# Gate and up begin with eight products of the first token half instead of four, in a fused encoder block on one Trainium2 core

## The chip, the core and the metric

The kernel runs on one core of a Trainium2 chip. The core has five engines, each with a queue of its own that it works off in order: TensorE (PE in the profile, and PEld for its weight loads), VectorE (DVE), ScalarE (ACT), GpSimd (POOL) and SyncE (SP), which here only issues DMAs. The engines meet through semaphores alone: an instruction that waits holds up everything behind it in its own queue. Matmuls write to PSUM, which has eight banks of 128 x 512 fp32; everything else lies in SBUF.

The metric is the device time of one launch in microseconds, a median over runs; lower is better.

## The reference, cut to what matters

```python
def reference(x, ...):                      # x: (1, 1024, 1024) float32
    h = rms_norm(x, norm1_g)
    z = h @ w_in                            # conv value and gate, q, k, v
    conv_out = conformer_conv(a, gate, ...) # 31 taps, layer norm, silu
    attn_out = neighbourhood_attention(rms_norm(q), rms_norm(k), v, rpb)
    x = x + concat([conv_out, attn_out]) @ w_out
    h = rms_norm(x, norm2_g)
    return x + (silu(h @ w_gate) * (h @ w_up)) @ w_down   # d_ff = 2816
```

The change touches the end of `@ w_out` and above all the beginning of the last line: the second norm and the two products `h @ w_gate` and `h @ w_up`.

## The kernel before, in words

All matmuls of fp32 data run as three products of fp32r halves. `split` (L106) makes the halves: ScalarE casts the source into `hi` (L107), and VectorE or GpSimd subtracts, `lo = src - hi` (L111); the argument `sub` says which of the two. `mac` (L113) then issues hi x hi, hi x lo and lo x hi (L115 to L117).

The text of the kernel is the order of the work. There is no scheduler: each engine's queue is what the Python calls append to it, and where work of one kind is to stand between matmuls, functions are put in the list `woven`, from which `weave()` takes one after each group of three matmuls.

**Output projection.** `proj` (L808) sums eight groups for one unit (m, h): eight row blocks m of the output, two token halves h of 512 tokens. Raw weights arrive by DMA in tiles of the tag R (`R`, L85; three buffers), are split by `take` (L152), and the order of loads is the list `chunks` (L137). `resid` (L865) adds the residual on VectorE and stores the result to DRAM by SP. `square`, `token_sums` and `token_rows` (L967 to L986) make the second norm's scale for a token half: squares on ScalarE, sums on GpSimd, a sum over partitions and a transpose on TensorE. `norm2` (L988) applies it on VectorE, reading the scale from PSUM.

**Gate and up, as Strassen-Winograd.** The product has 22 blocks i of 128 columns; for each, seven products m1 to m7 take the place of eight. One product (`product`, L1216) is four `mac`s, 12 matmuls of 512 columns. The weights of a block are raw tiles `raw_gu[i, 0]` and `raw_gu[i, 1]` (`load_gu`, L995, two DMAs of 512 KB), their sums `t_sums` (L1000, four VectorE sums) and the splits of the seven operands (`prep`, L1134). The token side has operands that all blocks share: A11 and A12 are the two halves of the normed first token half (`h2`); S3, A22, S2, S1 and S4 need the second token half. `left` (L1171) makes one of these for a k: a VectorE sum or difference in place in `xT` (L1179) and a split. For blocks 0 and 1 the seven products of both blocks are taken pair by pair, in the order of the list `products` (L1012): m1, m2 (only A11, A12), then m7 (S3), m4 (A22), m6 (S2), m5 (S1), m3 (S4). The other blocks follow one by one (L1017).

Products add up in PSUM banks: bank A takes m1 and m2, bank D m7 and m4, bank B m6, m5 and m3. Between two products of a bank, `evac` (L1241) reads the partial sum out on VectorE or ScalarE, so the next product into the same bank waits for that sum. The one for m6 is `u2` (L1249), for m7 and m5 L1258, for m3 L1262.

From block 4 on m1 (from block 6 on m2 too) is itself done by seven quarter products for two blocks at once (`part`, L1098; `prep_part`); the token operands for it are made beside the early products on GpSimd and VectorE by `tok_full`, `tok_sum` and `tok_split`, at product numbers given by the table `TOK` (L1091).

The loop at L1369 runs over `products`. After product n and its `evac` it calls `after[n]` (L1363), which holds the norm of the second half and `left`, and then `prep`, which takes tasks in the order of their numbers. As engines work in order, what `after[n]` appends stands ahead of what `prep` appends after it: a cast for a weight on ScalarE stands behind the casts of `left` issued in the same step.

Of the kernel before, what the change touches and what calls it, by code (L numbers as in the profile page):

```python
# [12 lines left out]
P = 128  # L13
# [57 lines left out]
def build(ctx, tc, a):  # L71
# [7 lines left out]
    def T(tag, shape, bufs, name, dt=F32):  # L79
        return sb.tile(shape, dt, tag=tag, bufs=bufs, name=name)  # L80
# [2 lines left out]
        return T("G", [P, 1024], 21, name, dt)  # L83

    def R(name):  # L85
        return T("R", [P, 1024], 3, name)

    def H(name, dt=F32):
        return T("H", [P, 4096], 7, name, dt)
# [2 lines left out]
        return T("st", [P, 512], 5, name, dt)  # L92

    def SM(name, n=8):
        return T("sm", [P, 8], 16, name)[:, :n]

    def mm(name):
        return ps.tile([P, 512], F32, tag="mm", bufs=4, name=name)
# [20 lines left out]
    def lr(w):  # L119
        return w[:, :512], w[:, 512:]  # L120
# [90 lines left out]
    def wo_dst(d, k0):  # L211
        def dst():
            if (d, k0 // 4) == (1, 1):
                if not woq:
                    woq.append(H(f"wo{d}{k0}", F32R))
                o = k0 % 4 * 1024
                hl = (woq[0][:, o:o + 1024], woq[0][:, o + 1024:o + 2048])
            else:
                hl = (G(f"wo{d}{k0}h", F32R), G(f"wo{d}{k0}l", F32R))
            for j in range(2):  # L220
                wo[d, k0 + j] = [w[:, j * 512:(j + 1) * 512] for w in hl]
            return hl
        return dst

    for d in range(2):
        for k0 in (4, 6, 0, 2):
            want(a["wo"][k0 * P:(k0 + 2) * P, d * 512:(d + 1) * 512].rearrange("(k p) m -> p k m", p=P),
                 f"wo{d}{k0}", wo_dst(d, k0), (pool,) * 4 if d == 0 and k0 < 4 else (pool,))


    hT = [[H(f"hT{h}{w}", F32R).rearrange("p (k s) -> p k s", s=512) for w in range(2)] for h in range(2)]
# [721 lines left out]
    for h, ms_ in ((0, range(4)), (1, (0, 1))):  # L953
        for k in CONV:
            for m in ms_:
                proj(m, h, (k,), None, 1 + (m + 1) % 2)
        for m in ms_:
            resid(m, h)
        if h == 0:
            take(2)  # L960
    for m in range(6, 8):
        load_xT(m)
    take(2)

    ssum, rn, rows = {}, {}, {}

# [42 lines left out]

    ORDER = ("m1", "m6", "m7", "m2", "m5", "m4", "m3")  # L1010
    ms = [m + h * QF for m in range(QF) for h in range(2)]
    products = [(i, p) for p in ("m1", "m2", "m7", "m4", "m6", "m5", "m3") for i in range(2)]  # L1012
    PARTS = {"m1": {-7: ("P1", "P6"), -5: ("P2", "P5", "P7"), -3: ("P3", "P4")},
             "m2": {-1: ("P1", "P6"), 0: ("P2", "P5", "P7"), 2: ("P3", "P4")}}
    FIRST_I = {"m1": 4, "m2": 6}
    parted = lambda i, p: i >= FIRST_I.get(p, FB)
    products += [(i, p) for i in range(2, FB) for p in ORDER if not parted(i, p)]  # L1017

# [4 lines left out]
            for o, g in at_.items() if parted(i, m) else ():  # L1025
                parts_at.setdefault(n0 + o, []).append((m, i, g))
    LEAD = {"load": 2, "P1": -2, "P6": -2, "P7": -2, "P4": -1}
    tasks = [(n, ip) for n, ip in enumerate(products)]
    for n, gs in parts_at.items():
        for m, i, g in gs:  # L1030
            tasks += [(n - LEAD[q] - 0.5, (m, i, q)) for q in (("load",) if "P1" in g else ()) + g if q in LEAD]
# [50 lines left out]
    def tok_split(m, n):  # L1082
# [3 lines left out]
        else:  # L1086
# [1 line left out]
            tok4[m, n] = [t[:, 0], t[:, 1]]  # L1088
        split(*tok4[m, n], tok_raw[m, g][:, c], (pool,))

    TOK = {6: (tok_full, "m1", 0), 8: (tok_full, "m1", 3), 9: (tok_full, "m1", 2), 10: (tok_full, "m1", 1),  # L1091
           11: (tok_sum, "m1", 1), 12: (tok_sum, "m1", 3), 15: (tok_sum, "m1", 2), 16: (tok_split, "m1", 2),
           17: (tok_sum, "m1", 4), 19: (tok_split, "m1", 1), 20: (tok_split, "m1", 3), 21: (tok_split, "m1", 4),
           22: (tok_full, "m2", 0), 23: (tok_full, "m2", 3), 25: (tok_full, "m2", 1), 27: (tok_full, "m2", 2),
           28: (tok_sum, "m2", 1), 30: (tok_sum, "m2", 3), 31: (tok_split, "m2", 3), 32: (tok_sum, "m2", 2),
# [38 lines left out]
    def prep(n=1, upto=None):  # L1134
        while tasks and (n > 0 if upto is None else tasks[0][0] <= upto):
            n -= 1
            job = tasks.pop(0)[1]
            if len(job) == 3:
                prep_part(*job)
                continue  # L1140
            i, p = job
            if i > 1 and p == ("m6" if parted(i, "m1") else "m1"):
                t_sums(i, (1, 2))
            elif i > 1 and p == ("m7" if parted(i, "m1") else "m6"):
                t_sums(i, (3, 4))
            b = {"m1": (0, 0), "m2": (0, 1), "m3": (1, 1)}.get(p)
            m = {"m5": 0, "m6": 1, "m7": 2, "m4": 3}.get(p)
            src = lr(raw_gu[i, b[0]])[b[1]] if b else lr(tsum[i, m // 2])[m % 2]
            top[i, p] = lr(G(f"t{i}{p}", F32R))
            split(*top[i, p], src, (dve,) if i < 2 and p in ("m1", "m2", "m6", "m5") else (pool,))  # L1150
            if (i, p) == (0, "m2"):
                load_gu(1, 1)
            if (i, p) == (1, "m7"):
                load_gu(2, 0)
            if (i, p) == (0, "m3"):
                load_gu(2, 1)
            if (i, p) == (1, "m3"):
                load_gu(3, 0)
            if i > 1 and p == ("m7" if parted(i, "m2") else "m2"):
                load_gu(i + 1, 1)  # L1160
            if i > 1 and p == "m3":
                load_gu(i + 2, 0)


    sop = {}
# [17 lines left out]
        norm2(k, 0)  # L1183
        split(h2[0][:, k], h2[1][:, k], xT[k][:, :512])

    for i, j in ((0, 0), (0, 1), (1, 0)):
        load_gu(i, j)

    units = [(m, 0) for m in range(4, 8)] + [(m, 1) for m in range(2, 8)]
    for m in range(4):  # L1190
        square(m, 0)
    beside = {(2, 5): [lambda: token_sums(0)], (3, 1): [lambda: token_rows(0)],
              (4, 5): [lambda: t_sums(0, (1, 2))], (5, 5): [lambda: t_sums(0, (3, 4))],
              (7, 3): [lambda: t_sums(1, (1, 2))], (7, 5): [lambda: t_sums(1, (3, 4))]}
    for kb, at_ in enumerate(((3, 3), (3, 7), (4, 3), (4, 7), (5, 3), (5, 7), (6, 3), (6, 7))):
        beside.setdefault(at_, []).append(lambda kb=kb: h2_one(kb))
    for m, h in units:
# [13 lines left out]

    sd = dr.tile([QF, P, 7 * 512], F32, name="sd")
    LEFT = {"m1": "A11", "m2": "A12", "m3": "S4", "m4": "A22", "m5": "S1", "m6": "S2", "m7": "S3"}
    gt, bank, sl, u2, late = {}, {}, {}, {}, []

    def product(i, p):  # L1216
        w = {"m1": "A", "m2": "A", "m7": "D", "m4": "D"}.get(p, "B")
        alone = p == "m2" and parted(i, "m1")
        first = p in ("m1", "m6", "m7") or alone
        if alone:  # L1220
            if i % 2 == 0:
                pair_sl[0] = lr(cv(f"A{i}"))
            bank[i, w] = pair_sl[0][i % 2]
        elif first:
            bank[i, w] = (tp if w == "D" and i > 1 else mm)(f"{w}{i}")
        acc, (th, tl), s = bank[i, w], top.pop((i, p)), sop[LEFT[p]]
        for k in range(HK):
            mac(acc, [q[:, k * P:(k + 1) * P] for q in (th, tl)], [s[h][k] for h in range(2)],
                k == 0 and first, k == HK - 1)
            weave()  # L1230
        return acc
# [9 lines left out]
    def evac(i, p, acc):  # L1241
        if p == "m1":
            gt[i] = G(f"g{i}")
        l, r = lr(gt[i])
        if p == "m1":
            (act.copy if i else dve.tensor_copy)(l, acc)
        elif p == "m6":
            u2[i] = ST(f"u2{i}")
            dve.tensor_tensor(u2[i], acc, l, OP.add)  # L1249
            if i < 2:  # L1250
                gate2(i, bank[i, "D"])
        elif p == "m2":
            sl[i] = ST(f"sl{i}") if i < 2 else acc
            if parted(i, "m1"):
                dve.tensor_tensor(acc, acc, l, OP.add)
            act.activation(sl[i], acc, AF.Silu)
        elif p in ("m5", "m7"):
            dve.tensor_tensor(r, acc, l if p == "m7" else r, OP.add)  # L1258
            if i < 2 and p == "m5":
                up2(i, r, bank[i, "D"])  # L1260
        elif p == "m3":
            dve.tensor_tensor(l, acc, l, OP.add)  # L1262
            dve.tensor_tensor(l, sl[i], l, OP.mult)
            keep(i, 0, l)
        elif i > 1:
            gate2(i, acc)
            late.append(lambda: up2(i, r, acc))
# [89 lines left out]
    def prep_items(n):  # L1357
        for _ in range(n):
# [1 line left out]
            n_prep[0] += 1  # L1360


    after = {0: lambda: (token_sums(1), act.activation(warm, eps, AF.Silu)),  # L1363
             1: lambda: [(norm2(k, 1), left("S3", k)) for k in range(HK)],
             2: lambda: [(norm2(k + HK, 1), left("A22", k)) for k in range(HK)],
             3: lambda: [left("S2", k, dve) for k in range(HK)],
             5: lambda: [left("S1", k) for k in range(HK)],
             7: lambda: [left("S4", k) for k in range(HK)]}
    for n, (i, p) in enumerate(products):  # L1369
        if n == 1:  # L1370
            woven.extend([lambda: None, lambda: token_rows(1)])
        pacc = product(i, p)
        evac(i, p, pacc)
        if n in after:
            after[n]()
        if late and p != "m4":
            late.pop(0)()
        due = extra and p in ("m2", "m5", "m7", "m6", "m3")[:5 if parted(i, "m2") else 4]
        if due and not parted(i, "m1"):
            extra.pop(0)()  # L1380
        for m, i0, g in parts_at.get(n, ()):
            for q in g:
                part(m, i0, q)
        if n < 6:
            prep((1, 1, 1, 1, 1, 1)[n])
        else:
            prep(upto=n + 4)
        if due and parted(i, "m1"):
            extra.pop(0)()
        if n in TOK:  # L1390
            TOK[n][0](*TOK[n][1:])
        if i == FB - 1 and p == "m7":
            for q in range(4):
                load_item(q)
        if i == FB - 1 and p in ("m5", "m4", "m3"):
            prep_items(1 + (p == "m5"))
# [103 lines left out]
```

## Time and profile before

| | |
|---|---|
| median of 3 runs | 1056.51 us (1055.28 to 1057.07) |
| the profiled execution: its time | 1057.38 us |
| the profiled execution: its span, first to last instruction | 1055.7 us |
| mean granted TensorE clock | 0.988 of full speed |
| TensorE busy | 1031.6 us, 98% |
| VectorE busy | 777.8 us, 74% |
| GpSimd busy | 490.5 us, 46% |
| ScalarE busy | 477.6 us, 45% |

The page of the profile has busy times by engine, and the span in 40 equal slices: a digit is the busy share of a slice in tenths, in the row PEclk the granted clock. The timelines list instructions of one engine by start and duration in us, with line, output and input tiles by the program's names; in brackets is the idle time just before, and what ended it. The table of waits lists which engine waited for which line of which other, in all, how often, and the longest. Matmuls are pipelined: one of 512 columns takes 0.39 us from start to end, and the next starts 0.23 us after it.

### The profile page before, as it was taken

To read this page: it belongs to the slowest core of one execution; us is meant where nothing else is said; L and a number is where in the kernel's file an instruction comes from. 1 tells how busy PE (TensorE), PEld (TensorE's weight loads), DVE (VectorE), ACT (ScalarE), POOL (GpSimd) and SP (SyncE) were. 2 spreads that over 40 slices of the span, in tenths; PEclk is the share of its full clock that TensorE was granted. 3 is DMA by queue.
4 is the path that set the end of the run, shared out by engine and by line. 5 is a ranking of instruction groups with operands and counts; after the bars stand their busy time and mean duration, and the time that the engine had idled before them with its cause. 6 is when DMAs were issued, how large, how long until landed. Compare 5 with 4: busy or idle time off the path is not lost.

```text
span 1055.7 us, 15166 instructions
## 1 busy us (share of the span) xinstructions
PE 1031.6 (98%) x5334; PEld 859.2 (81%) x5334; DVE 777.8 (74%) x1200; ACT 477.6 (45%) x1044; POOL 490.5 (46%) x380
## 2 busy tenths in 40 slices
PE   9999999999999899689999999999999999999998
PEld 8888888877787687468888888888888888888887
DVE  5789997887754157887778877877787667857885
ACT  7465349737865234324243333433333444433432
POOL 1036755524641545687786675666667200002320
PEclk9999999999999999789999999999999999999999
DMA  9335781338222512023343344434333598623641
GB/s 350 152 89 186 226 256 40 120 111 269 62 97 95 198 41 70 1 75 126 120 150 131 101 151 146 148 122 146 130 105 130 190 340 288 210 81 119 208 152 50
DMA packets 75084, 152.53 MB, mean 144 GB/s; under 512 B 13824, under 2 KB 22784, under 8 KB 74368
## 3 DMA queue, kind: packets, MB, share of 16 engines
q1 hardware_dynamic: 72992, 148.21, 41.7%
q10 hardware_dynamic: 2016, 3.36, 0.9%
q8 instruction: 42, 0.69, 0.3%
q14 instruction: 34, 0.28, 0.1%
HBM read 112.38 MB, written 44.76 MB: 149 GB/s over the span
## 4 chain that ended last, share of the span: by engine, by line
PE 88%; DVE 7%; ACT 2%; POOL 1%; issue 1%; DMA 1%; DVEq 0%; ACTq 0%; POOLq 0%
PE B L115 5%; PE B L116 5%; PE B L117 5%; PE z L115 4%; PE z L117 4%; PE z L116 4%; PE D L115 3%; PE D L116 3%; PE D L117 3%; PE gl L115 3%; PE gl L117 3%; PE gl L116 3%; PE p L720 2%; PE o L739 2%; PE s L680 2%; PE pj L117 2%
## 5 line engine op out<-in xcount | busy, mean ns | idle before, releaser
L363 DVE SCALAR_TENSOR_TENSOR cv<-u,par,cv 128x1009 f32<-128x1009 f32 (+14 forms) x92 | 117.4, 1277 | 2.3
L389 POOL TENSOR_TENSOR pa<-pa,pr 128x1022 f32<-128x1022 f32 (+5 forms) x24 | 58.0, 2416 | 48.4 <-ACT pr L388 35.8
L1443 POOL TENSOR_TENSOR ou<-ou,resm 128x512 f32<-128x512 f32 x8 | 12.6, 1582 | 143.5 <-DMA resm<-xd 141.6
L107 ACT CAST op<-sr 128x512 fp32r<-128x512 f32 x77 | 47.6, 619 | 58.1 <-PE B2d L117 26.7
L111 DVE TENSOR_TENSOR op<-sr,op 128x512 fp32r<-128x512 f32 x77 | 58.1, 755 | 16.3 <-ACT op L107 16.3
L709 POOL TENSOR_SCALAR e<-e,rs 128x288 f32<-128x288 f32 (+1 forms) x64 | 33.9, 545 | 41.9 <-DVE rs L707 40.1
L1007 DVE TENSOR_TENSOR ts<-gu,ts 128x512 f32<-128x512 f32 x44 | 51.9, 1181 | 0.8
L107 ACT CAST op<-wd 128x512 fp32r<-128x512 f32 x54 | 33.4, 619 | 29.1 <-DVE wd L1345 18.5
L698 ACT ACTIVATE e<-e,mx 128x288 f32<-128x288 f32 (+1 forms) x64 | 36.5, 572 | 18.8 <-DVE mx L693 16.9
L111 DVE TENSOR_TENSOR op<-wd,op 128x512 fp32r<-128x512 f32 x54 | 41.3, 764 | 1.2
L693 DVE CUSTOM_DVE_ANT_0 e<-s,tab 128x288 f32<-128x288 f32 (+1 forms) x64 | 28.7, 503 | 13.6 <-PE s L680 13.6
L1258 DVE TENSOR_TENSOR g<-D,g 128x512 f32<-128x512 f32 x22 | 15.2, 689 | 23.2 <-PE D L117 23.2
L867 DVE TENSOR_TENSOR xT<-pj,xT 128x512 f32<-128x512 f32 x16 | 10.6, 685 | 28.3 <-PE pj L117 28.3
L416 ACT ACTIVATE sq<-z,r 128x64 f32<-128x64 f32 x96 | 28.3, 328 | 4.7 <-PE z L117 4.7
L1235 ACT ACTIVATE D<-D 128x512 f32<-128x512 f32 x22 | 12.8, 582 | 35.3 <-DVE D L1234 35.3
L388 ACT ACTIVATE pr<-u,par 128x1022 f32<-128x1022 f32 (+5 forms) x24 | 27.0, 1137 | 1.6 <-ACT vs L446 1.2
L720 PEld LDWEIGHTS p<-ident,e 128*96 128x96 f32 (+1 forms) x192 | 20.5, 133 | 6.9 <-POOL e L709 6.3
L973 POOL TENSOR_TENSOR sq<-sq,sq 128x512 f32<-128x512 f32 x13 | 18.1, 1394 | 17.0 <-ACT sq L969 16.7
L115 PE MATMUL B2d<-op 128*128 128x512 f32 x66 | 25.8, 391 | 0.0
L116 PE MATMUL B2d<-op 128*128 128x512 f32 x66 | 25.7, 389 | 0.0
L117 PE MATMUL B2d<-op 128*128 128x512 f32 x66 | 25.7, 389 | 0.0
L739 PE MATMUL o<-e,vw 96*64 96x128 f32 (+1 forms) x384 | 24.7, 277 | 0.0
(1463 smaller groups left out, 3801.0 us busy)
## 6 DMA issues: line engine op xcount, KB each, us to landing
gu<-in_gu SPq DMA_DIRECT2D x44, 512.0 KB
sr<-sd SPq DMA_DIRECT2D x77, 256.0 KB
sd<-sd SPq DMA_DIRECT2D x22, 512.0 KB
wd<-in_wd SPq DMA_DIRECT2D x36, 256.0 KB
sd<-g SPq DMA_DIRECT2D x33, 256.0 KB
x<-in_x SPq DMA_DIRECT2D x8, 512.0 KB
xT<-in_xp SPq DMA_DIRECT2D x8, 512.0 KB
xd<-xT SPq DMA_DIRECT2D x16, 256.0 KB
```

The lines of the kernel that those rows point to most:

```text
L107: act.copy(hi, src)
L111: eng.tensor_tensor(*[w[..., sl] for w in (lo, src, hi.bitcast(F32))], OP.subtract)
L115: pe.matmul(acc, lh, rh, start=start, stop=False, skip_group_check=True)
L116: pe.matmul(acc, lh, rl, start=False, stop=False, skip_group_check=True)
L117: pe.matmul(acc, ll, rh, start=False, stop=stop, skip_group_check=True)
L363: dve.scalar_tensor_tensor(acc[:, o], uc[:, i], dwk[:, c, t:t + 1], acc[:, o], OP.mult, OP.add)
L389: pool.tensor_tensor(pa[:, o], pa[:, o], pr[:, o], OP.add)
L698: act.activation(e, e, AF.Exp, bias=mx.pop((i, hh)), scale=-1.0, accum_out=sums[i][:, hh:hh + 1])
L709: pool.tensor_scalar(es[i][:, hh], es[i][:, hh], rs[:, hh:hh + 1], 1.0, op0=OP.mult, op1=OP.mult)
L720: pe.transpose(pt[:m, g * P:(g + 1) * P], es[i][:, hh, g * m:(g + 1) * m], ident)
L739: pe.matmul(os_[s_][hh * HD:(hh + 1) * HD, hp], vw[cb, rh + g][:, c:c + HD], pTs[i][hh][:, g], start=g == 0, stop=g == 2)
L1007: dve.tensor_tensor(o, l, r, OP.subtract)
```

## The change

Six things are changed together.

- `products` begins with m1 and m2 of blocks 0 and 1 and then of blocks 2 and 3, eight products that need the first token half alone; the later list leaves those four out. Their weights are prepared by one task per product; the m3 splits of blocks 0 and 1 get numbers three lower.
- `after` moves with it: the norm and S3 stand behind product 2, the norm of the other rows and A22 behind 3, S2 behind 4, S1 behind 9 (the second m7), S4 behind 11. A22's subtraction goes from GpSimd to VectorE. The token sums and rows are woven into products 1 and 2.
- Four raw buffers instead of three: both tiles of blocks 0 and 1 are loaded at once, and the later loads are issued from two places in `prep`. To make room the small tiles go from 16 to 12.
- The second half of w_out (d = 1) is split by VectorE instead of GpSimd, and all four of its chunks are taken ahead of the residuals of (0, 1) and (1, 1).
- The B banks of blocks 0 and 1 are one tile in the two banks of the tag cv; the Silu results of blocks 2 and 3 go to SBUF.
- `t_sums` of block 1 stands two units of `woven` earlier, and `TOK` has its first entries three steps later.

```diff
@@ tiles
     def R(name):
-        return T("R", [P, 1024], 3, name)
+        return T("R", [P, 1024], 4, name)
...
     def SM(name, n=8):
-        return T("sm", [P, 8], 16, name)[:, :n]
+        return T("sm", [P, 8], 12, name)[:, :n]
@@ output projection
-                 f"wo{d}{k0}", wo_dst(d, k0), (pool,) * 4 if d == 0 and k0 < 4 else (pool,))
+                 f"wo{d}{k0}", wo_dst(d, k0), (pool,) * 4 if d == 0 and k0 < 4 else (dve,) if d == 1 else (pool,))
...
         if h == 0:
-            take(2)
+            take(4)
     for m in range(6, 8):
         load_xT(m)
-    take(2)
@@ order of the products and of their preparation
-    products = [(i, p) for p in ("m1", "m2", "m7", "m4", "m6", "m5", "m3") for i in range(2)]
+    products = [(i, p) for i0 in (0, 2) for p in ("m1", "m2") for i in (i0, i0 + 1)]
+    products += [(i, p) for p in ("m7", "m4", "m6", "m5", "m3") for i in range(2)]
...
-    products += [(i, p) for i in range(2, FB) for p in ORDER if not parted(i, p)]
+    products += [(i, p) for i in range(2, FB) for p in ORDER if not parted(i, p) and (i > 3 or p not in ("m1", "m2"))]
...
-    tasks = [(n, ip) for n, ip in enumerate(products)]
+    tasks = [(n - 3 * ((n < 18) and ip[1] == "m3"), ip) for n, ip in enumerate(products)]
...
-    TOK = {6: (tok_full, "m1", 0), 8: (tok_full, "m1", 3), 9: (tok_full, "m1", 2), 10: (tok_full, "m1", 1),
-           11: (tok_sum, "m1", 1), 12: (tok_sum, "m1", 3), 15: (tok_sum, "m1", 2), 16: (tok_split, "m1", 2),
+    TOK = {9: (tok_full, "m1", 0), 10: (tok_full, "m1", 3), 11: (tok_full, "m1", 2), 12: (tok_full, "m1", 1),
+           13: (tok_sum, "m1", 1), 14: (tok_sum, "m1", 3), 15: (tok_sum, "m1", 2), 16: (tok_split, "m1", 2),
@@ prep: loads
-            if (i, p) == (0, "m2"):
-                load_gu(1, 1)
...
-            if i > 1 and p == ("m7" if parted(i, "m2") else "m2"):
-                load_gu(i + 1, 1)
-            if i > 1 and p == "m3":
+            if p == ("m7" if i in (2, 3) or parted(i, "m2") else "m2"):
                 load_gu(i + 2, 0)
+            if p == "m3":
+                load_gu(i + 2, 1)
...
-    for i, j in ((0, 0), (0, 1), (1, 0)):
+    for i, j in ((0, 0), (0, 1), (1, 0), (1, 1)):
         load_gu(i, j)
...
-              (7, 3): [lambda: t_sums(1, (1, 2))], (7, 5): [lambda: t_sums(1, (3, 4))]}
+              (6, 4): [lambda: t_sums(1, (1, 2))], (6, 5): [lambda: t_sums(1, (3, 4))]}
@@ product, evac
+            if w == "B" and i < 2:
+                if i == 0:
+                    pair_b.extend(lr(cv("B01")))
+                bank[i, w] = pair_b[i]
...
-            sl[i] = ST(f"sl{i}") if i < 2 else acc
+            sl[i] = ST(f"sl{i}") if i < 4 else acc
@@ left operands
-    after = {0: lambda: (token_sums(1), act.activation(warm, eps, AF.Silu)),
-             1: lambda: [(norm2(k, 1), left("S3", k)) for k in range(HK)],
-             2: lambda: [(norm2(k + HK, 1), left("A22", k)) for k in range(HK)],
-             3: lambda: [left("S2", k, dve) for k in range(HK)],
-             5: lambda: [left("S1", k) for k in range(HK)],
-             7: lambda: [left("S4", k) for k in range(HK)]}
+    after = {1: lambda: act.activation(warm, eps, AF.Silu),
+             2: lambda: [(norm2(k, 1), left("S3", k)) for k in range(HK)],
+             3: lambda: [(norm2(k + HK, 1), left("A22", k, dve)) for k in range(HK)],
+             4: lambda: [left("S2", k, dve) for k in range(HK)],
+             9: lambda: [left("S1", k) for k in range(HK)],
+             11: lambda: [left("S4", k) for k in range(HK)]}
     for n, (i, p) in enumerate(products):
-        if n == 1:
-            woven.extend([lambda: None, lambda: token_rows(1)])
+        if n in (1, 2):
+            woven.extend([lambda: None, lambda n=n: (token_sums, token_rows)[n - 1](1)])
...
-        if n < 6:
-            prep((1, 1, 1, 1, 1, 1)[n])
+        if n < 8:
+            prep()
```

More of the change, by code (lines that the diff above doesn't have):

```diff
@@ L1141, in prep @@
             i, p = job
[L1142 to L1145, printed above, removed]
+            if i > 1 and p in ("m6", "m7"):
+                t_sums(i, (1, 2) if p == "m6" else (3, 4))
             b = {"m1": (0, 0), "m2": (0, 1), "m3": (1, 1)}.get(p)
@@ L1150, in prep @@
             split(*top[i, p], src, (dve,) if i < 2 and p in ("m1", "m2", "m6", "m5") else (pool,))
-            if (i, p) == (0, "m2"):
-                load_gu(1, 1)
[L1153 to L1158, printed above, removed]
-            if i > 1 and p == ("m7" if parted(i, "m2") else "m2"):
-                load_gu(i + 1, 1)
-            if i > 1 and p == "m3":
+            if p == ("m7" if i in (2, 3) or parted(i, "m2") else "m2"):
                 load_gu(i + 2, 0)
+            if p == "m3":
+                load_gu(i + 2, 1)
     sop = {}
@@ L1213, in build @@
     LEFT = {"m1": "A11", "m2": "A12", "m3": "S4", "m4": "A22", "m5": "S1", "m6": "S2", "m7": "S3"}
-    gt, bank, sl, u2, late = {}, {}, {}, {}, []
+    gt, bank, sl, u2, late, pair_b = {}, {}, {}, {}, [], []
     def product(i, p):
@@ L1224, in product @@
         elif first:
-            bank[i, w] = (tp if w == "D" and i > 1 else mm)(f"{w}{i}")
+            if w == "B" and i < 2:
+                if i == 0:
+                    pair_b.extend(lr(cv("B01")))
+                bank[i, w] = pair_b[i]
+            else:
+                bank[i, w] = (tp if w == "D" and i > 1 else mm)(f"{w}{i}")
         acc, (th, tl), s = bank[i, w], top.pop((i, p)), sop[LEFT[p]]
```

## The prediction, made before the changed kernel ran

> **What bounds the kernel now.** I read the page first: busy shares, then the 40 slices.
>
> ```profile
> PE 1031.6 (98%) x5334; PEld 859.2 (81%) x5334; DVE 777.8 (74%) x1200; ACT 477.6 (45%) x1044; POOL 490.5 (46%) x380
> PE   9999999999999899689999999999999999999998
> PEclk9999999999999999789999999999999999999999
> ```
>
> TensorE sets the time everywhere but in slices 13, 16 and 17; a slice is 26.4 us, so 16 and 17 are 422 to 475 us. There the granted clock falls too. Next the waits of TensorE from 400 to 500 us:
>
> ```profile
> PE D L115 <- DVE g L1258: 10.1, 1, 10.1
> PE B L115 <- DVE u L1249: 4.2, 1, 4.2
> PE ss L978 <- DVE sq L973: 1.2, 1, 1.2
> PE B L115 <- ACT t2m L107: 0.5, 1, 0.5
> ```
>
> So this stage waits for VectorE. The timeline of TensorE (start, duration, idle before in brackets) gives the place and the price:
>
> ```profile
> 413.52 0.39 PE L115 MATMUL A<-h,t0m 128*128 128x512 f32 x1
> 416.24 0.39 PE L115 MATMUL A<-h,t1m 128*128 128x512 f32 x1
> ...
> 424.37 0.40 PE L117 MATMUL D<-S,t1m 128*128 128x512 f32 x1
> 434.88 0.77 PE L115 MATMUL D<-A,t0m 128*128 128x512 f32 x1 [10.12 <-DVE g L1258]
> ...
> 448.21 0.39 PE L117 MATMUL B<-S,t1m 128*128 128x512 f32 x1
> 452.82 0.77 PE L115 MATMUL B<-S,t0m 128*128 128x512 f32 x1 [4.22 <-DVE u L1249]
> 457.79 0.39 PE L115 MATMUL B<-S,t1m 128*128 128x512 f32 x1
> ```
>
> A product (12 matmuls) takes 416.24 - 413.52 = 2.72 us. After the 4.22 us wait one took 457.79 - 452.82 = 4.97, so a long wait costs 2.25 more at half clock. What VectorE does meanwhile:
>
> ```profile
> 411.59 0.75 DVE L990 SCALAR_TENSOR_TENSOR xT<-xT,par,rw 128x512 f32<-128x512 f32 x1 [2.30 <-PE rw L986]
> 418.36 2.71 DVE L990 SCALAR_TENSOR_TENSOR xT<-xT,par,rw 128x512 f32<-128x512 f32 x4
> 423.40 1.76 DVE L1179 TENSOR_TENSOR xT<-xT,xT 128x512 f32<-128x512 f32 x1 [2.33 <-POOL A L111]
> 430.10 0.68 DVE L1179 TENSOR_TENSOR xT<-xT,xT 128x512 f32<-128x512 f32 x1
> 431.46 0.69 DVE L111 TENSOR_TENSOR S<-xT,S 128x512 fp32r<-128x512 f32 x1 [0.68 <-ACT S L107]
> 432.07 0.68 DVE L1179 TENSOR_TENSOR xT<-xT,xT 128x512 f32<-128x512 f32 x1
> 435.75 0.68 DVE L1258 TENSOR_TENSOR g<-D,g 128x512 f32<-128x512 f32 x1
> 444.49 4.69 DVE L1179 TENSOR_TENSOR xT<-xT 128x512 f32<-128x512 f32 x4
> 450.38 1.69 DVE L111 TENSOR_TENSOR t1m<-ts,t1m 128x512 fp32r<-128x512 f32 x1 [1.21 <-ACT t1m L107]
> 452.00 0.68 DVE L1249 TENSOR_TENSOR u<-B,g 128x512 f32<-128x512 f32 x1
> 457.99 0.69 DVE L1258 TENSOR_TENSOR g<-B,g 128x512 f32<-128x512 f32 x1 [3.26 <-PE B L117]
> ...
> 488.54 0.68 DVE L1238 TENSOR_TENSOR g<-D,g 128x512 f32<-128x512 f32 x1
> ```
>
> It is one chain: norm of the second half (411.59), left operands S3, A22, S2, sums of m7 (435.75), S1 and S4, last t1m split, the sum u (452.00) that lets m5 start. The same sum of two SBUF tiles takes 0.68 at 430.10 and 1.76 at 423.40; the POOL timeline says why:
>
> ```profile
> 414.90 5.96 POOL L111 TENSOR_TENSOR S<-xT,S 128x512 fp32r<-128x512 f32 x4 [2.45 <-ACT S L107]
> 422.06 5.90 POOL L111 TENSOR_TENSOR A<-xT,A 128x512 fp32r<-128x512 f32 x4
> ```
>
> POOL was at A22 until 427.96, and idle at 430.10. The Trainium skill, "SBUF — State Buffer", § Who interferes with whom, says that a VectorE instruction with two SBUF inputs and a GpSimd one exclude each other for a whole instruction. These two rows agree.
>
> **The change, part by part.** Times of after are given on the clock of this profile.
>
> *Splits of w_out's second half on VectorE.*
>
> ```profile
> 346.30 1.05 ACT L107 CAST wo10h<-wo10r 128x1024 fp32r<-128x1024 f32 x1 [5.63 <-DMA wo10r<-in_wo]
> 347.61 1.05 ACT L107 CAST wo12h<-wo12r 128x1024 fp32r<-128x1024 f32 x1 [0.26 <-DMA wo12r<-in_wo]
> 347.43 2.36 POOL L111 TENSOR_TENSOR wo10l<-wo10r,wo10h 128x1024 fp32r<-128x1024 f32 x1 [2.86 <-DMA wo12r<-in_wo]
> 347.40 0.50 PE L115 MATMUL pj<-cm,wo10h 128*128 128x512 f32 x1 [0.49 <-ACT wo10h L107]
> 349.85 0.50 PE L117 MATMUL pj<-cm,wo10l 128*128 128x512 f32 x1 [1.71 <-POOL wo10l L111]
> 352.19 0.50 PE L117 MATMUL pj<-cm,wo12l 128*128 128x512 f32 x1 [0.69 <-POOL wo12l L111]
> ```
>
> On VectorE the 1024 columns take some 1.3 us (twice 0.68) against 2.36. The cast ends at 347.35, so the wo10l matmul starts at 348.7, 1.15 earlier; wo12l is done at 348.66 + 1.3 = 350.0, before its use at 350.35. Gain 1.84. Behind these splits on VectorE stand the residuals of (0,1) and (1,1), and behind those, on SP, their stores and the loads of xT6, xT7 and the first weights, some 5 us later; xT6 is first read two units of 24 matmuls (10.9 us) on, which covers it.
>
> *Eight first products.* Four are moved ahead, none added: TensorE's sum is unchanged, only its waits move. Token sums and rows move one slot back:
>
> ```profile
> 373.67 0.95 PE L978 MATMUL ss<-one,sq 128*128 128x1 f32 x8
> 377.35 0.60 PE L986 MATMUL rw<-ident,r20r 128*128 128x128 f32 x4
> 377.98 1.41 DVE L990 SCALAR_TENSOR_TENSOR xT<-xT,par,rw 128x512 f32<-128x512 f32 x2 [1.13 <-PE rw L986]
> 403.65 0.39 PE L115 MATMUL A<-h,t0m 128*128 128x512 f32 x1
> ```
>
> Norm starts after one product, half a product, the sums, a product's worth and the rows: 403.65 + 2.72 + 1.36 + 0.95 + 2.72 + 0.63 = 412.03, less 1.84: 410.2 (before 411.59).
>
> *S3.* The eight instructions took 418.36 - 411.59 = 6.77; t3m1's split now runs on POOL beside one of them: +0.4 (0 to 1.1 for each one met). 417.4.
>
> *A22 on VectorE.* Before, four norms in 2.71 while POOL split. Now each norm is followed by its own split, and the next norm queues behind it. ScalarE first does S3's last cast, the cast of t2m2, a Silu and A22's cast, 4 x 0.55:
>
> ```profile
> 433.32 0.61 ACT L107 CAST t1m<-ts 128x512 fp32r<-128x512 f32 x1
> 455.98 3.51 DMA gu<-in_gu
> ```
>
> 419.6; split 0.85 (0.69 to 1.76); then three rounds of 0.75 + 0.66 + 0.69 = 2.1: 426.75. In return S2 no longer waits for POOL (2.33).
>
> *S2.* Rounds of 432.07 - 430.10 = 1.97; POOL is empty but for t3m2: +0.6 (0 to 1.1). To the last cast 4 x 1.97 - 0.69 + 0.6: 434.55.
>
> *The first m7.* In ScalarE's order t0m7's cast stands behind the S2 casts: 0.61, then POOL 1.4 (5.90 / 4 = 1.48, less without VectorE beside it): 436.55. So TensorE, through its eight products but for t3m2 (cast behind A22's, POOL split about 428.5), waits here for S2, though m7 reads S3: this is what is late next. Two m7 products, two matmuls of them early: 5.0, and half of 2.25 for the clock (0 to 2.25): 442.65. The second sum, 0.2 until the last matmul is out and 0.68: 443.5.
>
> *S1 and S4 behind the m7 sums.* From that sum to u took 452.00 - 436.43 = 15.6. The same instructions follow in the same order, but POOL now has the m3 splits and token tiles between S1 and S4: +0.6 (0 to 4 x 0.6, four sums at 1.76 instead of 4.69 / 4). u at 459.7, m5 0.82 later: 460.5. Before, with four more products, m5 would start at 452.82 + 10.88 = 463.7. Gain 3.2, the 1.84 included.
>
> *Behind u.* VectorE's list to the last sum of block 2 is 489.22 - 452.00 - 3.26 = 34.0 us of work. TensorE's nine products to that point now are 0.82 + 2.25 + 24.5 + 1.4 (two quarter parts, 12 half-width matmuls) = 29.0; before there were eleven. VectorE is thus up to 5.0 us late, while B takes m6, then m5 with one product between. Waits 0 to 5.0 against 0.54 before; as most sums have a product of slack I take 1.1: +0.6.
>
> *Costed at nothing.* Four raw buffers: gu20 and gu30 load behind t0m2 and t1m2 (3.51 us by the row above) and are needed some 10 us later; the stores on SP behind them have no reader soon. B01 in the two free banks, Silu tiles for four blocks, t_sums of block 1 earlier, later token tiles (until product 21): same instructions, beside TensorE. Twelve small tiles instead of 16: four score steps (three tiles each) hold them all; if not, a step waits for an older step's last reader, which no row prices and the range's ends leave room for.
>
> Sum: -3.2 + 0.6 = -2.6. The span of 1055.7 becomes 1053.1; the profiled run (1057.38) lay 0.87 above the median of 1056.51, so 1053.9 as a median. 0.2%, about what a measurement of this kernel can tell, is 2.1 us.
>
> **Rivals.** *Slower: VectorE and POOL meet.* Each sum of two SBUF tiles that meets POOL costs up to 1.1 more on the chain; 20 stand between norm and u. Against it: POOL has only four splits up to S2. For it: from S1 on POOL has more. Three more than I count eat the gain (3.3 against 2.6); five more give 1053.9 + 5.5 = 1059.4. By the rule on the shared port above this goes on for every such pair, which speaks against A22 on VectorE.
>
> *No change:* the wait only moves: 10.1 becomes waits for t3m2 and t0m7, 4.2 a longer wait for u. VectorE's work, which sets u, is not less. 1056.5.
>
> *Far better:* the waits do not add clock losses and VectorE keeps up: all terms at their low ends, 2.6 + 0.4 + 0.2 + 0.6 + 1.1 + 0.6 + 1.1 = 6.6: 1049.9.
>
> The clock term: "TensorE: Matmul & The Clock Gate", Part 1, of the Trainium skill has half rate after an idle window of about 3.4 us; the 4.22 us row agrees. The wait before m7 is estimated at 3 us, so by the page mostly none: 1.1 less, 1052.8, inside the forecast's own range.
>
> **How the numbers follow.** Forecast 0.50 (own range 1051.5 to 1056, 0.12 of it within 0.2%), slower 0.28, no change 0.15, far better 0.07. Faster 0.45, same 0.27, slower 0.28. Range 1049 to 1060: from beyond the low ends to the slower rival; with every term at its upper end it would be some 1064, left out.
>
> **What would show it.** Right: wo10l's wait about 0.8; no wait at ss; a wait for t3m2 and one for t0m7 before product 8; m5 waiting for u near 460; at 500 us TensorE without waits. Wrong: the product m7 waiting past 438, sums of S1 and S4 at 1.7 each, or waits over 2 us behind u.

## The result and the profile after

The changed kernel takes 1065.54 us (median; 1063.77 to 1065.95) against 1056.79 (1055.28 to 1057.26) for the kernel before, run beside it: 1.0082 times as long, 95% interval 1.0065 to 1.0100. It is slower, by 7 to 11 us. The forecast was 1053.9, and its range ended at 1060.

The profiled execution has a span of 1063.9 us (before 1055.7). The page's busy line, and its slices of TensorE and of its clock:

```profile
PE 1031.7 (97%) x5334; PEld 858.2 (81%) x5334; DVE 782.0 (73%) x1208; ACT 478.0 (45%) x1044; POOL 477.8 (45%) x372
...
PE   9999999999999997849999999999999999999998
...
PEclk9999999999999999879999999999999999999999
```

The work is the same: 5334 matmuls, and 1031.7 us busy against 1031.6. Counted from 0, slice 13 is healed; the weak slices are now 15 to 17 (399 to 479 us), the same stage as before and lower in sum. The waits of TensorE from 400 to 500 us (in total, times, longest):

```profile
PE B L115 <- DVE u L1244: 12.0, 2, 11.1
PE A L115 <- ACT g L1241: 11.0, 2, 6.5
PE B L115 <- DVE g L1253: 1.7, 2, 0.9
PE B L115 <- DVE g L1257: 0.8, 1, 0.8
```

The wait of D for g (10.1) is gone as meant. In its place stand 11.0 us in which bank A waits for `g` on ScalarE, which the forecast did not have, and the wait for `u` has grown from 4.2 to 12.0. TensorE's timeline shows where (here and below a timeline shows chosen rows alone, and rows between them are left out):

```profile
401.77 0.39 PE L115 MATMUL A<-h,t0m 128*128 128x512 f32 x1
...
419.28 0.39 PE L117 MATMUL A<-h,t3m 128*128 128x512 f32 x1
426.13 0.80 PE L115 MATMUL A<-h,t2m 128*128 128x512 f32 x1 [6.46 <-ACT g L1241]
435.12 0.80 PE L115 MATMUL A<-h,t3m 128*128 128x512 f32 x1 [4.52 <-ACT g L1241]
440.00 0.40 PE L115 MATMUL D<-S,t0m 128*128 128x512 f32 x1
453.39 0.39 PE L117 MATMUL B<-S,t0m 128*128 128x512 f32 x1
464.86 0.76 PE L115 MATMUL B<-S,t1m 128*128 128x512 f32 x1 [11.07 <-DVE u L1244]
471.19 0.48 PE L115 MATMUL B<-S,t0m 128*128 128x512 f32 x1 [0.88 <-DVE u L1244]
475.05 0.47 PE L115 MATMUL B<-S,t1m 128*128 128x512 f32 x1 [0.88 <-DVE g L1253]
478.83 0.50 PE L115 MATMUL B<-S,t0m 128*128 128x512 f32 x1 [0.78 <-DVE g L1253]
482.67 0.50 PE L115 MATMUL B<-S,t1m 128*128 128x512 f32 x1 [0.78 <-DVE g L1257]
```

Read it by products. m1 of block 3 ends at about 419.7. m2 of blocks 2 and 3, which add into the same bank A as m1, each wait until m1 has been copied out of it. The first m7 starts at 440.00. The first m6 (block 0) ends at 453.8, and then the *second m6* (block 1) waits 11.07 us for `u` of the first, although it adds into another half of B. From there to the last m3 of these two blocks every product into B waits 0.8 to 0.9 us for the sum of the one before. Before, the second m6 followed the first without a wait, and it was the first m5 that waited.

ScalarE's timeline gives the reason for the two waits of A:

```profile
424.46 0.62 ACT L107 CAST A<-xT 128x512 fp32r<-128x512 f32 x1 [1.42 <-DVE xT L989]
424.98 0.61 ACT L107 CAST t3m<-gu 128x512 fp32r<-128x512 f32 x1
425.50 0.58 ACT L1241 COPY g<-A 128x512 f32<-128x512 f32 x1
427.52 0.62 ACT L107 CAST S<-xT 128x512 fp32r<-128x512 f32 x1 [1.44 <-DVE xT L1169]
...
433.45 0.62 ACT L107 CAST S<-xT 128x512 fp32r<-128x512 f32 x1 [1.36 <-DVE xT L1169]
433.98 0.61 ACT L107 CAST t0m<-ts 128x512 fp32r<-128x512 f32 x1
434.50 0.58 ACT L1241 COPY g<-A 128x512 f32<-128x512 f32 x1
```

The copy `act.copy(l, acc)` of block 2 is issued behind A22's four casts, that of block 3 behind S2's, and each of these casts but the first of A22 waits for VectorE. So the moved products hang on the very chain that they were to fill. VectorE's and POOL's timelines show the rest of the chain:

```profile
410.16 0.75 DVE L989 SCALAR_TENSOR_TENSOR xT<-xT,par,rw 128x512 f32<-128x512 f32 x1 [2.85 <-PE rw L985]
...
425.11 0.69 DVE L111 TENSOR_TENSOR A<-xT,A 128x512 fp32r<-128x512 f32 x1 [0.69 <-ACT A L107]
...
434.10 0.69 DVE L111 TENSOR_TENSOR S<-xT,S 128x512 fp32r<-128x512 f32 x1 [0.68 <-ACT S L107]
442.94 0.69 DVE L1253 TENSOR_TENSOR g<-D,g 128x512 f32<-128x512 f32 x1 [8.15 <-PE D L117]
...
445.66 0.69 DVE L1253 TENSOR_TENSOR g<-D,g 128x512 f32<-128x512 f32 x1 [1.43 <-PE D L117]
446.27 3.59 DVE L1169 TENSOR_TENSOR xT<-xT,xT 128x512 f32<-128x512 f32 x4
...
454.44 6.77 DVE L1169 TENSOR_TENSOR xT<-xT 128x512 f32<-128x512 f32 x4
...
464.03 0.68 DVE L1244 TENSOR_TENSOR u<-B,g 128x512 f32<-128x512 f32 x1
```

```profile
453.93 1.71 POOL L111 TENSOR_TENSOR t0m<-gu,t0m 128x512 fp32r<-128x512 f32 x1
...
458.95 1.71 POOL L1075 TENSOR_TENSOR qtm<-h,h 128x512 f32<-128x512 f32 x1
```

VectorE now stands idle for 8.15 us, for a product that itself waited. S4's four sums take 6.77 us, against 4.69 before; beside them POOL runs the m3 splits and token tiles without a pause.

All of the loss lies in this stage: the first quarter product of block 4 (`q40m`), ahead of which the same number of products stands in both, starts at 488.50 before and 496.42 after, 7.9 us later, and the spans differ by 8.2. Counted from the start of the first product it is 488.50 - 403.65 = 84.85 us before and 496.42 - 401.77 = 94.65 after: the stage itself is 9.8 us longer, and the earlier start gives 1.9 of it back.

### The profile page after: what moved, and what is told of

Read it like the earlier page. It is cut to its first block, busy times and chain, and to the rows that moved or that the text cites. A ratio compares the mean times of both kernels' runs of the same rounds, so it can differ in the third digit from the quotient of the medians.

```text
span 1063.9 us, 15169 instructions
## 1 busy us (share of the span) xinstructions
PE 1031.7 (97%) x5334; PEld 858.2 (81%) x5334; DVE 782.0 (73%) x1208; ACT 478.0 (45%) x1044; POOL 477.8 (45%) x372
## 4 chain that ended last, share of the span: by engine, by line
PE 90%; DVE 6%; ACT 2%; issue 1%; POOL 0%; DMA 0%; SPq 0%; DVEq 0%; ACTq 0%; POOLq 0%
PE B L115 5%; PE B L116 5%; PE B L117 5%; PE z L115 4%; PE z L117 4%; PE z L116 4%; PE D L115 3%; PE D L116 3%; PE D L117 3%; PE gl L117 3%; PE gl L116 3%; PE gl L115 3%; PE pj L117 2%; PE pj L116 2%; PE pj L115 2%; PE p L720 2%
## 5 line engine op out<-in xcount | busy, mean ns | idle before, releaser
L1230 ACT ACTIVATE D<-D 128x512 f32<-128x512 f32 x22 | 12.8, 582 | 38.2 <-DVE D L1229 38.2
L720 PE MATMUL p<-ident,e 128*96 128x128 f32 (+1 forms) x192 | 24.4, 276 | 0.0
```

What stands on the lines that cost most here:

```text
L720: pe.transpose(pt[:m, g * P:(g + 1) * P], es[i][:, hh, g * m:(g + 1) * m], ident)
```

## The experiments

Three theories were set against each other. *Pair:* the two halves of the tile B01 are tied to each other. *Copies:* the copies of m1 stand behind casts in ScalarE's order. *VectorE:* its list of work sets the end, so that waits only move. Below, a version's change is given as its ratio to the kernel before, run beside it on the same chip. Each version has one trace. What stands ahead of the first product is the same in the changed kernel and in its versions, and yet the first product starts between 400.94 and 401.94 in their traces; so times of two traces are good to about 1 us, unless they are counted from that start.

**1. The pair taken out of the changed kernel, and put into the kernel before.**

```diff
 # e1_two_banks: the changed kernel
-                if i == 0:
-                    pair_b.extend(lr(cv("B01")))
-                bank[i, w] = pair_b[i]
+                bank[i, w] = tp(f"B{i}")
 # e4_before_pair: the kernel before
+            if w == "B" and i < 2:
+                if i == 0:
+                    pair_b.extend(lr(cv("B01")))
+                bank[i, w] = pair_b[i]
+            else:
...
```

> The changed kernel, but B of blocks 0 and 1 are two single-bank tiles in place of the two halves of the pair B01. Theory 'pair': each product into one half of the pair waits for VectorE's sum that reads the other half; without the pair the second m6 follows the first at about 453.8 us, the first m5 starts at about 464.9 instead of 471.2, and the four waits of 0.8 to 0.9 behind it shrink: 6.3 to 8.5 us less, 1057 to 1059.5. Rival 'VectorE': its list of sums and splits sets the end and the waits only move behind u: 1064 to 1066.

> The kernel before, with one edit: B of blocks 0 and 1 are the two halves of one pair tile, as in the changed kernel. Theory 'pair': the second m6 now waits for u of the first (near 452), the first m5 for u of the second, some 6 us later, and three or four waits of 0.8 follow: 6 to 9 us more, 1062.5 to 1065.5. Rival: the halves are two banks, so nothing changes: 1055.5 to 1057.5.

e1: 1059.58 us, ratio 1.0026 (1.0016 to 1.0036), where the changed kernel has 1.0082: 0.56% or 6.0 us less. e4: 1063.98 us, ratio 1.0068 (1.0055 to 1.0081): 7.2 us more than the kernel before, from this edit alone. TensorE's timeline of e1, then of e4:

```profile
453.00 0.39 PE L115 MATMUL B<-S,t1m 128*128 128x512 f32 x1
464.27 0.77 PE L115 MATMUL B<-S,t0m 128*128 128x512 f32 x1 [8.38 <-DVE u L1242]
```

```profile
453.44 0.77 PE L115 MATMUL B<-S,t1m 128*128 128x512 f32 x1 [7.15 <-DVE u L1254]
459.23 0.47 PE L115 MATMUL B<-S,t0m 128*128 128x512 f32 x1 [0.88 <-DVE u L1254]
```

With two tiles the second m6 starts at 453.00, when the first is out, and the first m5 at 464.27 instead of 471.19; the small waits are gone. With the pair in the kernel before, its second m6 waits, as in the changed kernel, and the wait of 0.88 us behind it appears too. The pair is shown as a cause, in both directions. In both kernels with the pair the profile names `u` of the first m6, on VectorE, as what released the second m6; with two tiles it shows no wait there. The edits also move B to other banks: the two tiles are of the tag `mm` in the kernel before and of `tp` in e1, the pair is of `cv`. But the sum that is waited for reads the other half alone, and the wait is absent in `mm` and in `tp`, so the bank by itself does not explain it. Why one tile in place of two brings the wait stays open: nothing here shows that the two halves would disturb each other on the chip; a version with the pair and without that wait was not tried.

**2. The copies of m1 ahead of the casts.** e2 issues A22 and S2 one product later and the weight splits ahead of them; e11 and e12 do one part each, all with the pair kept.

```diff
 # e2_copies_ahead has both hunks, e11_groups_later the first, e12_splits_first the others
-             3: lambda: [(norm2(k + HK, 1), left("A22", k, dve)) for k in range(HK)],
-             4: lambda: [left("S2", k, dve) for k in range(HK)],
+             4: lambda: [(norm2(k + HK, 1), left("A22", k, dve)) for k in range(HK)],
+             5: lambda: [left("S2", k, dve) for k in range(HK)],
@@
+        if 1 < n < 8:
+            prep()
         if n in after:
             after[n]()
@@
         if n < 8:
-            prep()
+            prep(n < 2)
```

> The changed kernel with the pair kept, but A22 and S2 issued one product later each and the weight splits issued ahead of them, so that ScalarE's copies of m1 of blocks 2 and 3 stand ahead of the casts of A22 and S2. Theory 'copies': the waits of 6.46 and 4.52 us for g go (under 1.5 left together), m7 starts by about 430 us instead of 440, S1 begins right behind S2 near 436 instead of 446, u comes near 454.5 instead of 464: 9 less, about 1056.5. Rival 'VectorE': its order keeps u near 464 whatever TensorE does before it: 1064 to 1066.

> The changed kernel (pair kept) with one part of the second edit: A22 and S2 issued one product later each, the weight splits left behind them. In ScalarE's order the copy for block 2 then stands ahead of A22's casts and the copy for block 3 ahead of S2's, but t1m7's cast stays behind S2's. Theory 'copies': the waits for g fall from 6.46 and 4.52 us to one of about 5.4, as with the whole edit (1058.6), and the second m7 waits 1 to 2 us for its split: 1058.5 to 1060.5. Rival 'splits': it is t0m7 and t1m7 behind S2's casts that hold m7, as the forecast had it: 1064 to 1065.5.

> The changed kernel (pair kept) with the other part of the second edit alone: the weight splits are issued ahead of S3, A22 and S2, these stay where they were, so t0m7's cast comes ahead of S2's, and both copies of m1 stay behind the casts of A22 and S2. Theory 'copies': both waits for g stay (6 to 7 and 4 to 5 us), 1064 to 1066. Rival 'splits': m7 starts near 432 and the time is 1058 to 1060.

e2: 1058.58 us, ratio 1.0020 (1.0012 to 1.0029), 6.5 us less than the changed kernel. e11: 1059.40, ratio 1.0032 (1.0022 to 1.0043). e12: 1063.94, ratio 1.0076 (1.0060 to 1.0093). The waits of TensorE for the copies in e11, then in e12:

```profile
PE A L115 <- ACT g L1241: 4.4, 1, 4.4
```

```profile
PE A L115 <- ACT g L1241: 10.0, 2, 6.8
```

The first m7 starts at 432.59 in e2, 431.97 in e11 and 438.51 in e12 (440.00 in the changed kernel). Counted from the first product that is 31.3, 30.9 and 37.1 us, against 38.2. So it is the copies and not the weight splits that held it. e2 gained less than the 9 us expected, as one wait for a copy was left (5.4 us, block 3), the second m7 sum stood behind a weight split until 439.09, and S1 and S4 then took 18.3 us again: `u` came at 457.4, not 454.5.

**3. Both edits.**

```diff
 # e3_both: the diffs of e1 and e2 together
```

> Both edits: two single-bank tiles for B of blocks 0 and 1, and the copies of m1 ahead of the casts of A22 and S2. Theories 'pair' and 'copies' together: the first m5 starts near 455 us and nothing waits long behind it: 1047 to 1050, under the kernel before. If the two losses overlap (one hides the other) it stays at 1055 to 1058. Rival 'VectorE': 1062 to 1066.

e3: 1052.73 us, ratio 0.9961 (0.9948 to 0.9975): faster than the kernel before, by 0.4%. From e1 to e3 it is 0.65% or 6.9 us, from e2 to e3 0.59% or 6.2 us, so the two losses hardly overlap: 6.0 + 6.5 us against the 12.8 us from the changed kernel to e3. It missed the expected 1047 to 1050; 5.4 and 9.4 us of waiting are left:

```profile
PE B L115 <- DVE u L1242: 9.4, 1, 9.4
PE A L115 <- ACT g L1239: 5.4, 1, 5.4
```

**4. What is left of the wait for u.** e5 takes S4, which only m3 reads, from ahead of `u`; e6 takes from POOL what it did beside S4's sums. Both build on e3.

```diff
 # e5_S4_behind_u
-             11: lambda: [left("S4", k) for k in range(HK)]}
+             13: lambda: [left("S4", k) for k in range(HK)]}
 # e6_pool_clear
-    tasks = [(n - 3 * ((n < 18) and ip[1] == "m3"), ip) for n, ip in enumerate(products)]
+    tasks = [(n, ip) for n, ip in enumerate(products)]
@@
-        if n in TOK:
-            TOK[n][0](*TOK[n][1:])
+        for t in {12: (9, 10, 11, 12)}.get(n, () if n < 12 else (n,)):
+            if t in TOK:
+                TOK[t][0](*TOK[t][1:])
```

> The version with both edits, and the left operand S4 (needed by m3 alone) issued behind the sums u of the two m6 instead of ahead of them. Theory 'order': what m5 waits for is only VectorE's place for u, 9.45 us late behind S4's four sums (6.79 us) and a split; u comes near 451 instead of 457.5, m5 starts near 451.6 instead of 458.3, and m3 waits 1 to 3 us for S4: 3.5 to 5.5 less than the version with both edits (1052.7), 1047 to 1049. Rival 'VectorE': its list of work sets the end, so the wait only moves to m3 and behind: 1052 to 1053.5.

> The version with both edits, with the m3 splits and the token tiles that POOL has between S1 and S4 issued behind S4. Theory 'meeting': S4's four sums took 6.79 us because POOL was at work beside each; without that they take 3 to 4.7, u comes 2 to 3 us earlier, time 1050 to 1051. Rival: POOL's own splits of S1 and S4 are met all the same and the m3 splits come late: 1052 to 1054.

e5: 1051.06 us, ratio 0.9949 (0.9934 to 0.9964), 1.3 us less than e3 by the ratios, whose intervals overlap; it lies between the two expected ranges. From the first product to `q40m` e5 takes 480.67 - 401.67 = 79.00 us and e3 482.15 - 401.32 = 80.83. e6: 1054.52, ratio 0.9983 (0.9974 to 0.9993), 2.3 us more than e3 and above both expected ranges. TensorE in e5, then VectorE in e6:

```profile
450.74 0.47 PE L115 MATMUL B<-S,t0m 128*128 128x512 f32 x1 [1.18 <-DVE u L1242]
461.64 0.77 PE L115 MATMUL B<-S,t0m 128*128 128x512 f32 x1 [5.20 <-DVE g L1251]
```

```profile
448.48 3.56 DVE L1169 TENSOR_TENSOR xT<-xT 128x512 f32<-128x512 f32 x4
...
454.86 0.68 DVE L1242 TENSOR_TENSOR u<-B,g 128x512 f32<-128x512 f32 x1
...
463.77 1.73 DVE L1080 TENSOR_TENSOR qtm<-qtm 128x512 f32<-128x512 f32 x1 [5.96 <-POOL qtm L1075]
465.43 0.68 DVE L1251 TENSOR_TENSOR g<-B,g 128x512 f32<-128x512 f32 x1
```

In e5 the wait for `u` falls from 9.45 to 1.18, and 5.20 us of waiting comes back two products later: the sum of the first m5 now stands behind S4's sums on VectorE. Here the rival 'VectorE' is mostly right. In e6, S4's sums take 3.56 us instead of the 6.79 of e3: the meeting with POOL is real and had cost 3.2. The rule that the prediction took from "SBUF — State Buffer", § Who interferes with whom, of the Trainium skill agrees with these rows. But a token sum on VectorE, ahead of the sum of m5, now waits 5.96 us for POOL's late tiles, and TensorE's m3 with it (3.26 us).

**5. Single parts of the change.** e7 is the kernel before with the splits of w_out alone; e8 is e3, and e10 the changed kernel, with A22's subtraction back on POOL.

```diff
 # e7_before_wo
-                 f"wo{d}{k0}", wo_dst(d, k0), (pool,) * 4 if d == 0 and k0 < 4 else (pool,))
+                 f"wo{d}{k0}", wo_dst(d, k0), (pool,) * 4 if d == 0 and k0 < 4 else (dve,) if d == 1 else (pool,))
@@
-            take(2)
+            take(4)
     for m in range(6, 8):
         load_xT(m)
-    take(2)
 # e8_A22_pool (on e3), e10_after_A22_pool (on the changed kernel)
-left("A22", k, dve)
+left("A22", k)
```

> The kernel before with the one edit that the splits of w_out's second half are on VectorE (and all four weight pieces are taken before the loads of xT6 and xT7). The first product starts 1.9 us earlier, as in the changed kernel (401.77 against 403.65). Theory: the stage behind is a chain from the norm on, so the gain is kept, 1.5 to 2 us: 1054.3 to 1054.8. Rival: the chain starts from VectorE's last squares, which do not move: 1056 to 1056.5.

> The version with both edits, with A22's subtraction back on POOL. If VectorE's ping-pong with ScalarE (A22 from 419.5 to 427.4) is what sets S2, POOL lets the four norms go first but holds S2's first sum: by the kernel before S2's first sum waited 2.33 us for POOL; S2 ends 0 to 2 us later, time 1052.7 to 1055. Rival 'meeting': VectorE is freed of four splits of 0.7 to 1.6, the chain is shorter by 1 to 3: 1050 to 1051.7.

> The changed kernel with one part undone: A22's subtraction is on POOL again. ScalarE's casts of A22 then need not wait for VectorE's turns, so the copy for block 2 comes near 421 instead of 425.5 and its wait of 6.46 us falls to about 2; the copy for block 3 stays behind S2's casts, whose end moves by less than 1 us, so the second wait takes most of it. Theory 'copies': the m7 start moves little, 1064 to 1065.5. Rival 'A22 on VectorE': its four turns cost what they add to the chain, 1.2 to 3 us: 1062.5 to 1064.

e7: 1053.98 us, ratio 0.9973 (0.9964 to 0.9983), 2.9 us less than the kernel before, a little over the 1.5 to 2 expected. The kernel before with this one part of the change beats it. e8: 1051.54, ratio 0.9955 (0.9938 to 0.9971), 0.6 us less than e3 by the ratios, whose intervals overlap. In e8 no wait for a copy is left, but two others take its place (2.6 and 2.2 us, shown in the last section), and `u` comes hardly earlier. TensorE, then VectorE:

```profile
424.15 0.39 PE L115 MATMUL D<-S,t0m 128*128 128x512 f32 x1
```

```profile
455.86 0.68 DVE L1242 TENSOR_TENSOR u<-B,g 128x512 f32<-128x512 f32 x1
```

In e3 these rows start at 432.27 and 457.48. Counted from the first product, the first m7 of e8 is 7.7 us earlier and `u` 1.2. So the 5.4 us that e3 still waits for a copy are little of what e3 lacked to its expected time: without them TensorE waits for VectorE's sum and POOL's split instead.

e10: 1062.58, ratio 1.0055 (1.0039 to 1.0072), 2.9 us less than the changed kernel by the ratios, whose intervals overlap a little; from the first product to `q40m` it takes 492.98 - 401.05 = 91.93 us against 94.65. In e10 TensorE has these waits:

```profile
420.81 0.50 PE L115 MATMUL A<-h,t2m 128*128 128x512 f32 x1 [1.86 <-ACT g L1241]
432.01 0.80 PE L115 MATMUL A<-h,t3m 128*128 128x512 f32 x1 [6.97 <-ACT g L1241]
```

Only the first wait shrinks, as expected. But S2's last split now starts at 430.99 instead of 434.10, and the second copy comes 3.1 us earlier with it (0.7 of that stands ahead of the first product). The expectation of theory 'copies', that S2's end would move by less than 1 us, was wrong, and the time lies in the range of its rival: A22's turns on VectorE (splits at 418.95, 421.04, 423.07, 425.11 in the changed kernel, each waiting for a cast that waits for a norm) are longer than POOL's way, although there S2's first two sums take 1.76 and 1.75 beside POOL.

**6. All that helped.**

```diff
 # e9_all: e3 with the edits of e5 and e8
```

> The version with both edits, with A22's subtraction on POOL and S4 issued behind the two u. If the two gains (1.2 and 1.7 us by the version with each alone) are of different waits they add: 1052.7 - 2.9 = 1049.8, between 1049 and 1050.5. If the later one only waits where the first has been (the first m3 for the sum behind S4, 5.2 us), it stays at 1050.5 to 1051.5.

e9: 1049.68 us (1049.51 to 1049.86), ratio 0.9934 (0.9919 to 0.9948), 7 us under the kernel before and some 16 under the changed kernel. From e3 it is 0.27% or 2.9 us, no less than the gains of e5 and e8 together (1.3 and 0.6), which alone are not clear of the noise; from the first product to `q40m` it takes 478.35 - 401.48 = 76.87 us, 4.0 less than e3. What it still waits for longest is the sum behind S4:

```profile
449.30 0.47 PE L115 MATMUL B<-S,t0m 128*128 128x512 f32 x1 [0.72 <-DVE u L1242]
460.21 0.77 PE L115 MATMUL B<-S,t0m 128*128 128x512 f32 x1 [5.22 <-DVE g L1251]
```

## Why the prediction was wrong

The forecast span was 1053.1, the measured one 1063.9, 10.8 us more. Its own marks split this up: 2.8 at the end of the second m7 sum (446.35 against 443.5), 1.5 from there to the start of `u` (17.7 against 16.2), 6.3 from `u` to the first m5 (7.16 against 0.82), and 0.1 behind. Of its signs of being wrong, m7 past 438 came (440.00), and sums at 1.7 us came for S4 (6.77 for four) but not for S1 (3.59).

- *Splits of w_out.* Right. The first product starts at 401.77, 1.88 us earlier (1.84 forecast); that the two agree so closely is partly chance, as versions with the same beginning start it between 400.94 and 401.94. e7 shows that the gain is kept to the end.
- *Norm, S3, A22, S2.* Right within a microsecond: norm at 410.16 (410.2), A22's last split out at 425.80 (426.75), S2's last cast out at 434.07 (434.55). What the prediction did not price is A22 on VectorE against A22 on POOL: 2.9 us in the changed kernel (e10) and 0.6 in e3 (e8), both with intervals that overlap.
- *"TensorE, through its eight products but for t3m2".* This step failed first. The prediction looked at the weight splits that feed the moved products and not at what empties the bank between m1 and m2 of a block. The copies on ScalarE were behind the casts of A22 and S2, and TensorE waited 6.46 and 4.52 us. It had named a late engine for this place, t0m7's cast behind S2's; moving that cast and the other weight splits alone (e12) changed the start of m7 from 440.00 to 438.51, moving the copies (e11) to 431.97. Against the forecast the step cost 2.8 us; against what the order could give, 6 to 7.
- *S1 and S4 behind the m7 sums.* Mechanism right, size wrong: the meeting of VectorE and POOL was taken at +0.6 with an upper end of 2.4, and S4's sums alone went from 4.69 to 6.77, 2.1 more; less the 0.6 that is the 1.5 us above. The slower rival rested on this. It was right in the sign of the result largely by luck, as the meeting explains 1.5 of the 10.8 us. Its count was off too: between the norm and `u` VectorE has not 20 but 28 instructions with two inputs in SBUF (16 sums, 12 subtractions of splits).
- *"Costed at nothing: B01 in the two free banks".* This is the largest miss. The prediction asked whether the banks were free, and not whether one tile in place of two joins their waits. e1 and e4 give 6.0 and 7.2 us for it.
- *Behind u.* VectorE keeps up. In e1 and e3, without the pair, no wait over 0.5 us follows the first m5 up to 500 us. The 1.1 us taken there was not far off, and no wait of TensorE from 400 to 520 us in the changed kernel points to the four raw buffers, the Silu tiles or the twelve small tiles; they were not taken away one by one.
- *The clock term.* The sum took half of 2.25 us for the slow matmuls behind the wait ahead of m7. In the changed kernel both m7 run at full clock (matmuls of 0.39 us); the slow matmuls stand in the two m2 ahead of them, behind the waits of 6.46 and 4.52 us. The last section shows how little regular this price is.

With the two missed waits repaired, e3 takes 1052.73 us, near the forecast. This is partly chance: e2's edit also removes the wait for t0m7 that the forecast had (second m7 sum out at 439.77, 3.7 us before the forecast's), and the way from there to `u` takes 1.5 of that back (`u` at 457.48, 2.2 before).

## What to carry to other kernels

When products are moved ahead to fill a gap, follow each of them to the end: not only what feeds it, but what must empty its bank before the next one adds into it, and behind which casts that copy stands on its in-order engine. Two banks given as halves of one tile were one thing to wait for in this program, so look for readers of the other half. And a gap filled in front of a chain leaves the chain as long as it was: in e8 the first m7 came 7.7 us earlier than in e3, and `u` 1.2. What shortened the chain here was taking work out of it (S4 behind `u` and A22's subtraction back on POOL, 2.9 us together), while the other way of helping it, clearing POOL, brought a new wait.

## What the runs showed of the chip that was not expected

The granted clock can fall after a wait of 2.60 us. TensorE's timeline of e8 has such a wait, some microseconds behind one of 2.21:

```profile
429.69 0.51 PE L117 MATMUL D<-S,t1m 128*128 128x512 f32 x1 [2.21 <-POOL t1m L111]
...
434.89 0.75 PE L115 MATMUL D<-A,t0m 128*128 128x512 f32 x1 [2.60 <-DVE g L1251]
435.44 0.63 PE L116 MATMUL D<-A,t0m 128*128 128x512 f32 x1
...
438.45 0.39 PE L117 MATMUL D<-A,t0m 128*128 128x512 f32 x1
```

The matmuls after it take 0.63 us instead of 0.39, for some 3.2 us; the granted clock is 0.52 from 434.8 to 438.2 us and 1.00 from 420 us up to there. Behind the wait of 2.21 alone the matmuls were at full speed. "TensorE: Matmul & The Clock Gate", Part 1, of the Trainium skill puts the fall behind an idle window of about 3.4 us; this row does not agree. How long the slow stretch lasts does not follow the wait, either: in the changed kernel it ends after 7 matmuls behind the wait of 6.46 us (at 429.3), after 10 behind that of 4.52 (at 439.6), and not within the 12 behind that of 11.07. So one long wait costs less than one product's 2.25 us, or all of it, and nothing in these rows tells beforehand which.
